# Moving the split weights and the split coefficients to other byte offsets, step by step, in a one-core PEER and mixer kernel

## The chip, the core and the metric

One core of a Trainium2 chip runs the whole kernel as one program. The time is the device time of one execution in microseconds; the kernel before took 1731.04 us, the median of three runs (1727.76, 1731.04, 1736.29).

## The reference, cut to what matters

256 tokens of width 1024 pass through a first block (a mixer, a cross attention, a PEER layer) and a second one (an even mixer, a gated feed-forward, an odd mixer, a second feed-forward). The change lies in the PEER layer. There each token picks, for each of 8 heads, 16 of 128 x 128 experts; an expert is one row of `expert_down` and one of `expert_up`:

```python
u = expert_down[eidx]
a = jax.nn.gelu(jnp.einsum('thkd,td->thk', u, xb), approximate=False)
coef = (g * a.astype(jnp.float32)).astype(xb.dtype)
return jnp.einsum('thk,thkd->td', coef, expert_up[eidx])
```

The kernel computes it densely: for all 16384 experts it takes the product with the token, applies gelu, multiplies with a gate that is zero for the experts not chosen, and multiplies the result with `expert_up`.

## The kernel before, in words

**Three products for one.** Every large product is made in float32r from split operands: a weight piece `raw` (128 partitions x 1024 float32, 4096 bytes in each partition) is loaded by a DMA of SyncE's queue (L418), ScalarE copies it to `hi`, rounded (L430), and VectorE subtracts to get `lo` (L431). The other operand is kept in two halves in the same way. TensorE then makes hi x hi, hi x low half and lo x hi.

**The two expert stages.** In the *down* stage there are 128 steps, one for each first key j. A step (`proj_b`) takes the piece `down[j]` and makes 8 x 3 matmuls (L440, L441, L442): the stationary operand is a 128-column slice of `hi`, `hi`, `lo`; the moving one is the token block `xh`, `xl`, `xh`, 256 columns wide. ScalarE applies gelu (L1207, or L1217 later). In the first part of this stage other work is laid between the steps: first the top-16 search on VectorE, then 64 groups of gate products (L1184 to L1196), which end with 16 small bf16 and fp16 matmuls each (L1192, L1193). In the *output* stage there are again 128 steps (`out_step`, 8 x 3 matmuls at L582, L583, L584): the stationary operand is a slice of `hi`, `hi`, `lo` of `up[j]`; the moving one is the split coefficient of key j, `ch`, `cl`, `ch`, 256 columns each. A coefficient pair (two keys) is made by multiplying gate and gelu (L1244, with gelu values fetched from DRAM, L1243) and splitting (L435, L436) into the tile `u3`.

**Order.** Each engine runs its instructions in a fixed order, and waits on semaphores for the others. A weight tile has three buffers in the expert stages, so a piece is loaded, split and used up to three steps apart.

**Places.** What the change moves is where operands start within a partition. In this text a *place* is the start address in bytes modulo 256. In the kernel before all `raw`, `hi` and `lo` tiles are 4096 bytes long, so that in every buffer of every pool they have one place; in the built program it is 128. The tiles of the moving operands have these places, from the layout of the built program: `xh` and `xl` of the first block and of the down stage 192 and 192; `uh`, `ul` of the pool `xu` (memory projections, PEER queries, even and odd output) 64 and 64, and `u3` 64, so that `ch` and `cl` are at 64 and 64; the token block of the first feed-forward `xh` 64 and `xl` 192, its split activations `uh`, `ul` 64 and 64; the token block of the second feed-forward `xh` 128 and `xl` 0, its `uh`, `ul` 0 and 0. The pools lie one behind the other: `small`, `xu`, a gap of 64 bytes, `w0` (three weight buffers, used in all stages), then `w1` or `w2` (two or three more buffers outside the expert stages), then what a stage needs. A tag's slot has the size of the largest tile with this tag. `skip` puts a small tile in front of a pool and has GpSimd fill it (L399).

Of the kernel before, what the change touches and what calls it, by code (L numbers as in the profile page):

```python
# [11 lines left out]
F32R = mybir.dt.float32r  # L12
# [360 lines left out]
class Builder:  # L373
    def __init__(self, tc, nc, A, out, stages=None):
        self.tc, self.nc, self.A, self.out = tc, nc, A, out
        self.stages = stages
        self.flip = 0
        self.gate = None
        self.free = 100
        self.later = []  # L380
        self.mark = None

    def pool(self, ctx, name, bufs=1, space=None, side=None):
# [13 lines left out]
    def skip(self, pool, nbytes):  # L397
        t = pool.tile([P, nbytes // 4], F32, tag="skip", name="skip", bufs=1)
        self.nc.gpsimd.memset(t, 0.0)  # L399

    def act_set(self, name):
        self.tc.keep_in_program_order(self.nc.scalar.preload_act_table_set(name))
# [7 lines left out]
    def weight(self, ap, width=D, parts=1):  # L410
        nc = self.nc
        i = self.wn % sum(n for _, n in self.wps)
        self.wn += 1
        wp, bufs = self.wps[0] if i < self.wps[0][1] else self.wps[1]
        raw = wp.tile([P, D], F32, tag="raw", name="raw", bufs=bufs)
        cuts = [slice(i * width // parts, (i + 1) * width // parts) for i in range(parts)]
        for c in cuts:
            nc.sync.dma_start(raw[:, c], ap[:, c])  # L418
        hi = wp.tile([P, D], F32R, tag="hi", name="hi", bufs=bufs)
        lo = wp.tile([P, D], F32R, tag="lo", name="lo", bufs=bufs)  # L420
        with ExitStack() as ctx:
            if self.gate:
                self.free -= 1
                if self.free < 0:
                    for ins in self.gate:
                        ctx.enter_context(self.tc.issue_after(ins))
                if self.free < -4:
                    self.gate = None
            for c in cuts:
                nc.scalar.activation(hi[:, c], raw[:, c], AF.Copy)  # L430
                nc.vector.tensor_sub(lo[:, c], raw[:, c], hi[:, c].bitcast(F32))  # L431
        return hi, lo

    def split(self, hi, lo, src):
# [213 lines left out]
    def build(self):  # L648
# [17 lines left out]
        with ExitStack() as ctx:  # L666
# [24 lines left out]
            cw = ExitStack()  # L691
            self.wps = [(base, 3), (self.pool(cw, "w1"), 2)]
            with ExitStack() as c1:
# [32 lines left out]
            with ExitStack() as c2:  # L726
                self.wps = [(base, 3), (self.pool(c2, "w2"), 3)]
                self.op, self.ot = self.xu, "u"
# [352 lines left out]
    def peer(self, xu, base, cw, cx, cq, late, spill, nxt):  # L1081
        nc, A = self.nc, self.A
        mm = nc.tensor.matmul
        with ExitStack() as ctx:
# [119 lines left out]
            while j < P and work:  # L1204
                a = acts_next()
                for i in range(2):
                    self.run(self.proj_b(x, A["down"][j + i], lambda ps: nc.scalar.activation(a[:, i], ps, AF.Gelu),  # L1207
                                         self.tp))
# [5 lines left out]
            for j in range(kept, P):  # L1214
                def ev(ps):
# [3 lines left out]
                    nc.vector.tensor_mul(s, s, a)  # L1219

                self.run(self.proj_b(x, A["down"][j], ev, self.tp))
            cq.close()
# [3 lines left out]
            self.consts(LATE, "c_late")  # L1226
            u1 = self.xu.tile([P, 8, T], F32R, tag="uh", name="u3")
            order = [j for j in range(0, P, 2) if j >= kept] + [j for j in range(GA, P, 2) if j < kept]
# [3 lines left out]
            def step(n):  # L1232
                j = order[n // 2]
                if n % 2 == 0:
# [6 lines left out]
                    if j < kept:  # L1241
                        a = acts_next()
                        nc.sync.dma_start(a.rearrange("p i t -> p (i t)"), store[j // 2])  # L1243
                        nc.vector.tensor_mul(src, src, a)  # L1244
                    i = 4 * (n // 2 % 2)
                    ch, cl = u1[:, i:i + 2], u1[:, i + 2:i + 4]
                    self.split(ch, cl, src)
# [3 lines left out]

            after = Lazy(nxt)
            self.out_proj(step, P, self.h, after, tail=2)
        return after.get()

# [495 lines left out]
```

## Time and profile before

| | before |
|---|---|
| median of three runs | 1731.04 us (1727.76 to 1736.29) |
| profiled execution, its own time | 1739.33 us |
| its span, first to last instruction | 1737.6 us |
| TensorE matmul, busy | 1683.0 us, 97% |
| weight loads, busy | 1602.0 us, 92% |
| VectorE, busy | 1241.1 us, 71% |
| ScalarE, busy | 873.8 us, 50% |
| mean granted TensorE clock | 0.989 |
| down stage (from its first step to the first output step) | 302.40 to 700.74 us |
| output stage (first step to its end) | 700.74 to about 1072 us |

A matmul of 256 columns is listed with about 280 ns, but successive ones start 113 to 119 ns apart, because they overlap. So the busy share says that TensorE always had something in work, and not how fast the stream went. The starts tell that: a step of 24 matmuls lasts from the start of its first one to the start of the next step's first one. Lines are those of the kernel before.

### The profile page before, as it was taken

The numbers are of one execution on the slowest core, as the hardware profiler recorded it, in microseconds if no ns is written. First come the engines' busy times: TensorE is split into PE (matmuls) and PEld (weight loads), VectorE is DVE, ScalarE is ACT, GpSimd is POOL, SyncE is SP. The second block draws the span as 40 slices with busy tenths as digits, with TensorE's granted clock in tenths as the row PEclk, the third lists the DMA queues.
The fourth block names the chain that finished last, engine by engine and source line by source line (L and its number), as shares of the span: only waits on it lengthen the run. The fifth ranks groups of instructions, "written<-read, shape, count | busy, mean of one in ns | idle before, by whom it ended". The sixth has DMA issues, their size and how long they took to land.

```text
span 1737.6 us, 33082 instructions
## 1 busy us (share of the span) xinstructions
PE 1683.0 (97%) x13220; PEld 1602.0 (92%) x13220; DVE 1241.1 (71%) x2309; ACT 873.8 (50%) x1358; POOL 89.1 (5%) x246
## 2 busy tenths in 40 slices
PE   7999999999999999999999999899999999999999
PEld 6879889999999999989999999678999987799998
DVE  6686559998798985678555556686777765677775
ACT  6445345545455554444444446464555454455543
POOL 1011010000000000000000000401100010210000
PEclk9999999999999999999999999999999999999999
DMA  7434454577555655889655556443455544345551
GB/s 263 152 104 147 146 172 131 187 236 260 175 186 199 194 196 188 309 289 299 190 189 186 185 189 210 157 135 110 162 192 186 191 159 155 102 162 190 188 188 62
DMA packets 97516, 318.03 MB, mean 183 GB/s; under 512 B 11841, under 2 KB 13505, under 8 KB 96850
## 3 DMA queue, kind: packets, MB, share of 16 engines
q1 hardware_dynamic: 89154, 301.39, 53.1%
q10 hardware_dynamic: 8208, 14.52, 2.2%
q8 instruction: 104, 1.70, 0.4%
q14 instruction: 50, 0.41, 0.1%
HBM read 299.36 MB, written 16.52 MB: 182 GB/s over the span
## 4 chain that ended last, share of the span: by engine, by line
PE 70%; DVE 7%; DMA 3%; POOL 2%; issue 2%; ACT 1%; SPq 0%; POOLq 0%; DVEq 0%; ACTq 0%
PE tp L440 11%; PE tp L441 11%; PE tp L442 11%; PE acc L582 8%; PE acc L583 8%; PE acc L584 8%; PE acc L440 3%; PE acc L441 3%; DMA u<-store 3%; PE acc L442 3%; DVE lo L431 2%; PE tp L1192 1%; PE tp L1193 1%; DVE ga L1244 1%; DVE w L1345 1%
## 5 line engine op out<-in xcount | busy, mean ns | idle before, releaser
L430 ACT ACTIVATE hi<-raw 128x1024 fp32r<-128x1024 f32 (+1 forms) x533 | 560.2, 1057 | 660.8 <-PE tp L441 246.6
L431 DVE TENSOR_TENSOR lo<-raw,hi 128x1024 fp32r<-128x1024 f32 (+1 forms) x533 | 646.7, 1219 | 309.5 <-ACT hi L430 309.2
L440 PE MATMUL tp<-xh,hi 128*128 128x256 f32 x1680 | 476.7, 284 | 0.6 <-ACT u L1207 0.6
L441 PE MATMUL tp<-xl,hi 128*128 128x256 f32 x1680 | 471.8, 281 | 0.0
L442 PE MATMUL tp<-xh,lo 128*128 128x256 f32 x1680 | 471.1, 280 | 0.6 <-DVE lo L431 0.6
L442 PEld LDWEIGHTS tp<-xh,lo 128*128 128x128 f32 x1680 | 317.1, 189 | 0.8 <-DVE lo L431 0.8
L440 PEld LDWEIGHTS tp<-xh,hi 128*128 128x128 f32 x1680 | 317.0, 189 | 0.8 <-ACT u L1207 0.8
L441 PEld LDWEIGHTS tp<-xl,hi 128*128 128x128 f32 x1680 | 317.2, 189 | 0.0
L583 PE MATMUL acc<-u,hi 128*128 128x256 f32 x1024 | 288.4, 282 | 5.6 <-DVE u L436 5.6
L584 PE MATMUL acc<-u,lo 128*128 128x256 f32 x1024 | 288.2, 281 | 1.4 <-DVE lo L431 1.4
L582 PE MATMUL acc<-u,hi 128*128 128x256 f32 x1024 | 287.9, 281 | 0.0
L583 PEld LDWEIGHTS acc<-u,hi 128*128 128x128 f32 x1024 | 193.0, 188 | 6.4 <-DVE u L436 6.4
L584 PEld LDWEIGHTS acc<-u,lo 128*128 128x128 f32 x1024 | 196.9, 192 | 1.8 <-DVE lo L431 1.8
L582 PEld LDWEIGHTS acc<-u,hi 128*128 128x128 f32 x1024 | 193.0, 189 | 0.0
L440 PE MATMUL acc<-hi,xh 128*128 128x512 f32 (+1 forms) x256 | 103.5, 406 | 1.6 <-ACT y L479 1.6
L441 PE MATMUL acc<-lo,xh 128*128 128x512 f32 (+1 forms) x256 | 101.7, 397 | 0.5 <-DVE lo L431 0.5
L442 PE MATMUL acc<-hi,xl 128*128 128x512 f32 (+1 forms) x256 | 101.1, 395 | 0.0
L582 PE MATMUL acc<-uh,hi 128*128 128x256 f32 x352 | 98.3, 280 | 0.1
L583 PE MATMUL acc<-ul,hi 128*128 128x256 f32 x352 | 98.1, 279 | 0.0
L584 PE MATMUL acc<-uh,lo 128*128 128x256 f32 x352 | 98.1, 279 | 0.0
L457 POOL TENSOR_SCALAR rs_g<-rs_m 128x2 int32<-128x2 int32 (+2 forms) x20 | 10.2, 510 | 1263.8 <-DVE fq L296 810.3
L582 PE MATMUL acc<-oh,hi 128*128 128x256 f32 x256 | 73.1, 285 | 0.0
(436 smaller groups left out, 2801.8 us busy)
## 6 DMA issues: line engine op xcount, KB each, us to landing
raw<-down SPq DMA_DIRECT2D x128, 512.0 KB, 3.7
raw<-up SPq DMA_DIRECT2D x128, 512.0 KB, 4.4
raw<-ffn_up SPq DMA_DIRECT2D x88, 512.0 KB, 3.5
raw<-ffn_down SPq DMA_DIRECT2D x44, 512.0 KB, 3.4
raw<-even_in SPq DMA_DIRECT2D x28, 512.0 KB, 4.4
store<-u ACTq DMA_DIRECT2D x55, 256.0 KB, 3.4
u<-store SPq DMA_DIRECT2D x55, 256.0 KB, 4.7
raw<-odd_in SPq DMA_DIRECT2D x24, 512.0 KB, 3.5
```

Source lines behind the costliest of these rows:

```text
L430: nc.scalar.activation(hi[:, c], raw[:, c], AF.Copy)
L431: nc.vector.tensor_sub(lo[:, c], raw[:, c], hi[:, c].bitcast(F32))
L440: mm(out, lh, rh, start=start, stop=False)
L441: mm(out, lh, rl, start=False, stop=False)
L442: mm(out, ll, rh, start=False, stop=stop)
L582: mm(out, wh[:, cs], oh, start=start and j == 0, stop=False)
L583: mm(out, wh[:, cs], ol, start=False, stop=False)
L584: mm(out, wl[:, cs], oh, start=False, stop=stop and j == 1)
L1192: mm(o, p1[:, b, :, e], hi[:, b, :, e], start=True, stop=False)
L1193: mm(o, p1[:, b, :, e], lo[:, b, :, e], start=False, stop=True)
L1244: nc.vector.tensor_mul(src, src, a)
L1345: nc.vector.match_replace(out=w, in_to_replace=val[:, :8], in_values=s, imm_value=-3e38)
```

## The change

`weight` gives `hi` 64 and `lo` 48 elements more room in pools with three buffers, if `self.lines` is set, and takes its 1024 columns from an offset within that room. In the down stage `line_pair(j)` sets these offsets: that of `hi` goes through eight multiples of 32 bytes, a new one at each step, that of `lo` through seven, a new one every eighth step. In the output stage the offsets are multiples of 64 bytes: `hi` changes every fourth pair of keys, `lo` every sixteenth. `u3` becomes one row of 2144 elements, with `ch` always at one place in either half and `cl` at one of four places, 64 bytes apart, a new one for each pair. `w1` and `w2` get a 64-byte `skip` in front.

From the sizes: a slot of `hi` in `w0` grows from 4096 to 4352 bytes, one of `lo` from 4096 to 4288, the slot of `uh` and `u3` in `xu` from 8192 to 8576.

```diff
+    def skipped(self, ctx, name):
+        pool = self.pool(ctx, name)
+        self.skip(pool, 64)
+        return pool
...
-        hi = wp.tile([P, D], F32R, tag="hi", name="hi", bufs=bufs)
-        lo = wp.tile([P, D], F32R, tag="lo", name="lo", bufs=bufs)
+        if self.lines is None or bufs < 3:
+            hi = wp.tile([P, D], F32R, tag="hi", name="hi", bufs=bufs)
+            lo = wp.tile([P, D], F32R, tag="lo", name="lo", bufs=bufs)
+        else:
+            hi, lo = [wp.tile([P, D + m], F32R, tag=n, name=n, bufs=bufs)[:, o:o + D]
+                      for n, o, m in zip(("hi", "lo"), self.lines, (64, 48))]
...
+    def line_pair(self, j):
+        return tuple(8 * ((v - 4) % 8) for v in (j % 8, (j // 8 % 7 + 4) % 8))
...
-            self.wps = [(base, 3), (self.pool(cw, "w1"), 2)]
+            self.wps = [(base, 3), (self.skipped(cw, "w1"), 2)]
...
-                self.wps = [(base, 3), (self.pool(c2, "w2"), 3)]
+                self.wps = [(base, 3), (self.skipped(c2, "w2"), 3)]
...
                 for i in range(2):
+                    self.lines = self.line_pair(j + i)
                     self.run(self.proj_b(x, A["down"][j + i], lambda ps: nc.scalar.activation(a[:, i], ps, AF.Gelu),
                                          self.tp))
...
+                self.lines = self.line_pair(j)
                 self.run(self.proj_b(x, A["down"][j], ev, self.tp))
...
-            u1 = self.xu.tile([P, 8, T], F32R, tag="uh", name="u3")
+            u1 = self.xu.tile([P, 2144], F32R, tag="uh", name="u3")
...
-                    i = 4 * (n // 2 % 2)
-                    ch, cl = u1[:, i:i + 2], u1[:, i + 2:i + 4]
+                    m = n // 2
+                    self.lines = tuple(16 * ((v - 2) % 4) for v in (m // 4 % 4, m // 16))
+                    wide = u1[:, 1088 * (m % 2):1088 * (m % 2) + 1056 + 32 * (1 - m % 2)]
+                    o = 512 + 16 * ((m - 1) % 4)
+                    ch = wide[:, :512].rearrange("p (i t) -> p i t", i=2)
+                    cl = wide[:, o:o + 512].rearrange("p (i t) -> p i t", i=2)
...
             self.out_proj(step, P, self.h, after, tail=2)
+            self.lines = None
```

## Rows read from the trace of the kernel before

**Rows 1.** The page: busy time, and the chain that ended last.
```profile
PE 1683.0 (97%) x13220; PEld 1602.0 (92%) x13220; DVE 1241.1 (71%) x2309; ACT 873.8 (50%) x1358; POOL 89.1 (5%) x246
...
PE 70%; DVE 7%; DMA 3%; POOL 2%; issue 2%; ACT 1%; SPq 0%; POOLq 0%; DVEq 0%; ACTq 0%
```

**Rows 2.** Busy time by stretch (columns in the heading row), down stage then output stage.
```profile
core 0: us, PE busy (x) PEld busy (x) DVE busy (x) ACT busy (x) POOL busy (x), PEclk, DMA share, GB/s
302.30:401.40 99.10, 97.85 (x827) 97.24 (x826) 92.62 (x350) 49.88 (x73) 0.00 (x0) 1.00 0.68 228
401.40:652.70 251.30, 251.30 (x2368) 248.86 (x2367) 221.32 (x473) 140.14 (x291) 0.00 (x0) 1.00 0.60 195
652.70:700.70 48.00, 48.00 (x410) 48.00 (x409) 27.92 (x36) 23.68 (x36) 0.00 (x0) 1.00 0.59 187
700.70:808.50 107.80, 100.75 (x842) 99.55 (x841) 80.46 (x102) 46.26 (x53) 0.00 (x0) 0.98 0.89 306
808.50:1072.00 263.50, 263.29 (x2235) 262.96 (x2233) 147.06 (x152) 122.79 (x142) 0.00 (x0) 1.00 0.62 198
```

**Rows 3.** Timeline of TensorE: starts of steps far apart, in both expert stages.
```profile
652.69 0.28 PE L440 MATMUL tp<-xh,hi 128*128 128x256 f32 x1
...
697.91 0.28 PE L440 MATMUL tp<-xh,hi 128*128 128x256 f32 x1
...
808.51 0.28 PE L582 MATMUL acc<-u,hi 128*128 128x256 f32 x1
...
1065.73 0.28 PE L582 MATMUL acc<-u,hi 128*128 128x256 f32 x1
```

**Rows 4.** Timeline of TensorE in the output stage, 751 to 811 us: restarts and steps.
```profile
754.21 0.39 PE L583 MATMUL acc<-u,hi 128*128 128x256 f32 x1 [2.31 <-DVE u L436]
...
756.93 0.28 PE L582 MATMUL acc<-u,hi 128*128 128x256 f32 x1
...
759.65 0.28 PE L582 MATMUL acc<-u,hi 128*128 128x256 f32 x1
...
763.28 0.38 PE L584 MATMUL acc<-u,lo 128*128 128x256 f32 x1 [0.52 <-DVE lo L431]
...
765.98 0.28 PE L582 MATMUL acc<-u,hi 128*128 128x256 f32 x1
...
768.80 0.28 PE L582 MATMUL acc<-u,hi 128*128 128x256 f32 x1
```

**Rows 5.** Timeline of TensorE, first feed-forward: output step, then two input steps.
```profile
1244.78 0.28 PE L582 MATMUL acc<-uh,hi 128*128 128x256 f32 x1
...
1247.51 0.28 PE L440 MATMUL tp<-xh,hi 128*128 128x256 f32 x1
...
1250.33 0.28 PE L440 MATMUL tp<-xh,hi 128*128 128x256 f32 x1
...
1253.15 0.28 PE L582 MATMUL acc<-uh,hi 128*128 128x256 f32 x1
```

**Rows 6.** Timeline of TensorE: one output step of the second feed-forward.
```profile
1561.38 0.28 PE L582 MATMUL acc<-uh,hi 128*128 128x256 f32 x1
...
1564.23 0.28 PE L440 MATMUL tp<-xh,hi 128*128 128x256 f32 x1
```

**Rows 7.** Timeline of TensorE: end of the even mixer's output, four steps of matmuls.
```profile
1210.99 0.28 PE L582 MATMUL acc<-oh,hi 128*128 128x256 f32 x1
...
1221.87 0.28 PE L440 MATMUL acc<-xh,hi 128*128 128x256 f32 x1
```

**Rows 8.** Who waited for whom between 401 and 652 us.
```profile
ACT hi L430 <- PE tp L441: 106.7, 73, 2.3
DVE u L1184 <- PE tp L1193: 18.9, 43, 0.8
```

**Rows 9.** GpSimd's fills of skip tiles, by line: count, then min/median/max ns.
```profile
L399 POOL MEMSET skip<- x6: 104/111/118, 0.7 to 1516.7; 128x16 f32 x3, 128x8 f32 x2, 128x24 f32 x1
```

More of the change, by code (lines that the diff above doesn't have):

```diff
@@ L1253, in peer @@
             self.out_proj(step, P, self.h, after, tail=2)
+            self.lines = None
         return after.get()
```

## The prediction

> **What bounds the kernel now.** I read the page first, then busy time by stretch, then the starts of single matmuls. The page puts TensorE at 97% busy and gives it 70% of the chain that ended last; no other engine has over 7% of that chain [rows 1]. By stretch the two expert stages are TensorE's nearly throughout: all 251.30 us of the second part of the down stage, all 48.00 of its end, 263.29 of 263.50 us of the long part of the output stage, at a granted clock of 1.00, the 2.4 GHz level [rows 2]. Busy time can't show whether this stream could go faster, since matmuls overlap. So I count steps of 24 matmuls between two starts. From 652.69 to 697.91 us there are 16 steps, 2.826 us each; from 808.51 to 1065.73 us there are 91, 2.827 us each [rows 3]. That is 117.8 ns a matmul.
>
> This is not the best that the stream does. Between 756.93 and 759.65 us a step of the same stage, same tiles, same places, takes 2.72 us, 113.3 ns a matmul; the one from 765.98 to 768.80 takes 2.82 again [rows 4]. The end of the even mixer's output takes 10.88 us for 96 matmuls, 113.3 ns [rows 7]. So there are two paces, a fast one of 2.720 us and a slow one of 2.827 us a step, 0.107 us apart. What sets them? Two things, by the rows. One is how the stream starts: in the output stage the pace changes only at a wait. It is fast after the restart at 754.21 us and slow after the one at 763.28 [rows 4]; of six restarts there, four were followed by fast steps. The other is place: in the first feed-forward no wait lies between the steps, and yet the output step, whose two moving operands have one place, takes 2.73 us, and the input steps around it, with moving operands at 64 and 192, take 2.82 us, every time [rows 5]. At places 0 and 0 an output step takes 2.85 us [rows 6].
>
> In the expert stages nearly all steps are slow: in the down stage 2 of 128 are fast, in the output stage 12 of 128, all 12 between 751 and 808 us.
>
> **The change part by part.** *Moved operands.* No instruction of TensorE, ScalarE or VectorE in the expert stages is added or removed, none changes its shape, and no DMA changes its size or order. What changes is the place of the weights against the moving operands: `hi` gets a new one at each step of the down stage and every eighth step of the output stage, `cl` one every second step of that stage. The stream's relation, locked for 91 steps now, is then broken again and again. I price a step at one of the two paces, 2.720 or 2.827 us, and ask how many of them will be fast.
>
> Which steps can pay: in the down stage TensorE is busy to the end, and VectorE, with 221.32 of 251.30 us [rows 2], has 30 us in which a faster TensorE isn't held up. It already waits for TensorE's gate products 43 times, 18.9 us [rows 8], so it would start earlier too. From 302 to 401 us VectorE has 92.62 of 99.10 us; 30 steps gain at most 3.2 us there, and 6.5 us are free. So 128 steps of the down stage pay. In the output stage the first 35 steps, 700.70 to 808.50 us, lie in a stretch with a DMA share of 0.89 and 306 GB/s, against 0.62 and 198 after it [rows 2]; TensorE waits there for coefficients whose gelu values come by DMA [rows 4]. What TensorE saves there goes into that wait, and I count it at nothing; were that cover gone it would be up to 23 slow steps x 0.107 = 2.5 us. The other 93 pay. Together 221 steps.
>
> How many turn fast: none can turn below 2.720 us by any row, so the end of the range on one side is 221 x 0.107 = 23.6 us gained; if all went at the worst pace of these rows, 2.85 us [rows 6], 221 x 0.023 = 5 us are lost. For the share I have these: four of six restarts in the output stage; 1 of 64 or so among the restarts after the gate products in the down stage, which are all alike; one of the two places in the first feed-forward; none of those in the second. I take a third, between these ends and nearest to the places without a wait, since a new place without a wait is what the change makes. 221 / 3 = 74 steps, 2 of which are fast already: 72 x 0.107 = 7.7 us gained.
>
> *The rest of the kernel.* The diff moves more than it names. The slot of `uh` in `xu` grows by 384 bytes, so `ul` behind it goes from place 64 to 192, and all of `w0` from 128 to 0; its `lo` buffers then lie 4288 bytes apart and get places 0, 192 and 128. The growth of `w0`, 3 x 256 + 3 x 192 = 1344 bytes, with 384 and the new skip of 64, is 1792, seven times 256, so that everything behind `w1` or `w2` keeps its place. Outside the expert stages three of five or six weight buffers thus have a new place against their moving operands, and the pair in `xu` becomes one of 64 and 192, like the token block of the first feed-forward, which is slow [rows 5]. At stake are some 45 fast steps there (22 output steps of the first feed-forward at 2.73 us, the ends of the even and odd outputs [rows 7], the memory projections and some queries), 45 x 0.107 = 4.8 us if all are lost; and about 200 slow ones, which at the same third would gain 7 us. I take 2 us lost, nearer to the loss, as the pair in `xu` alone carries about 20 of the fast steps (20 x 0.107 = 2.1).
>
> *Added.* Two fills of 64 bytes by GpSimd, 0.11 us each [rows 9]. One stands at the start and one after the output stage, ahead of GpSimd's next work; GpSimd is 5% busy [rows 1]. Nothing; uncovered 0.2 us.
>
> *A rule against the trace.* The rows show two paces, 113.3 and 117.8 ns, at one clock [rows 3, 4]. The Trainium skill (SBUF — State Buffer, Specifications) says that SBUF has 16-byte lines and that an access pays when it crosses to a new one. All places here are multiples of 32 bytes, so by that rule each operand starts on a line as before, and the change gains and loses nothing. Likewise TensorE: Matmul & The Clock Gate (Back-to-back issue gap) gives columns over 2.4 GHz plus 2.5 ns, an estimate of 109 ns for 256 columns at any place, which none of these rows reaches. What would follow from places without effect is the first rival.
>
> **The sum.** 7.7 gained less 2 lost is 5.7 us. Against the profiled execution (1739.33 us, its span 1737.6 with 1.7 around it) that is 1733.6; against the median of the three runs, 1731.04, which lies 8.3 lower, 1725.3. The runs are compared by their medians, so I predict 1725.
>
> **The rivals.** *Place decides nothing, the start of a stream does.* For it: the same places ran at both paces in the output stage [rows 4], and the restarts of the down stage are alike. Against it: the first feed-forward changes pace with place, without a wait [rows 5]. The stages stay slow: 1731, within 3.
>
> *Odd places cost.* Every matmul operand read here in float32r starts at a multiple of 64 bytes now. In the down stage `hi` and `lo` go through multiples of 32, and half of these are odd. If a slice that starts in the middle of 64 bytes takes an access more, and the step falls behind by one more notch of the same 0.107 us, then steps with an odd `hi` or an odd `lo`, 96 of 128, lose 10.3 us, with nothing to cover it, since TensorE is busy throughout [rows 2]. With the 2 us of the other stages, and nothing gained in the even steps, that is 1743. It decides as soon as an odd step loses more than 0.03 us: a third of the output stage's 93 steps and the 32 even ones gains 4.5 us, of which the other stages leave 2.5, and 2.5 over 96 is 0.026. Against it: no row shows such a step, at any pace over 2.85.
>
> *Nearly all turn fast:* each new place shakes the stream out of the slow relation, as four of six restarts did. 200 x 0.107 = 21 less 2: 1712. Against it: the second feed-forward, where two relations alternate and neither is fast [rows 6].
>
> **How the numbers follow.** Forecast 0.48, its own range 1719 to 1734 (a half of the 221 fast with nothing lost elsewhere, a tenth with 4.8 us lost); place without effect 0.27; odd places cost 0.20; nearly all fast 0.05. About 0.5%, 8.7 us, is what a measurement of this kernel can tell from no change: faster means under 1722.4, slower over 1739.7. The forecast gives a little under half of its chance to faster, as its share need be only 0.46 instead of a third for that; with the last rival and a little of the others 0.31. Slower is most of the odd places' 0.20 and a little of the others: 0.20. The rest, 0.49, is within. The range from 1713 to 1745 leaves out about one in six.
>
> **What would show it.** Right: in the output stage after 810 us, steps of 2.72 and 2.83 us in blocks that change with the places, and the same mixed step by step in the down stage; more wait for DMA between 700 and 808 us. Wrong: all steps at 2.83 (first rival); steps over 2.85 us at odd places (second); or fast steps lost outside the expert stages by more than 4.8 us, by the first feed-forward's output steps going to 2.83. A change of instruction order on any engine, or a longer split on ScalarE or VectorE, would upset the argument as a whole.

## The result: 0.6% slower, and two profiles that do not show it

The changed kernel took 1743.97 us (median of 12 runs, 1740.00 to 1750.36), the kernel before 1733.32 us beside it (12 runs, 1726.54 to 1742.28): a ratio of 1.0064, interval 1.0042 to 1.0085, so 10.7 us slower. The prediction was 1725 us, on the other side, with 0.20 on slower. One run of all those named below, of the kernel before beside experiment 12 (1748.14 us), lay in a slower state of the chip and is left out.

The page of the profile after, busy time and the chain that ended last, to be laid beside [rows 1]:

```profile
PE 1687.5 (97%) x13220; PEld 1606.8 (92%) x13220; DVE 1241.9 (71%) x2309; ACT 873.9 (50%) x1358; POOL 89.4 (5%) x248
...
PE 69%; DVE 8%; DMA 3%; POOL 3%; issue 2%; ACT 1%; SPq 0%; POOLq 0%; ACTq 0%; DVEq 0%
```

TensorE has the same 13220 matmuls, and the two added fills of GpSimd are there (246 to 248 instructions). The span is 1738.2 us against 1737.6. These two profiles differ by 0.6 us where the medians differ by 10.7: the profiled execution of the kernel before took 1739.33 us, 6.0 over that kernel's median, and that of the kernel after 1740.00, 4.0 under its own. How far one execution of a kernel lies from another turns out to be half of the story below.

Busy time by stretch (columns as in [rows 2]), the kernel after:

```profile
401.40:652.70 251.30, 251.30 (x2361) 248.75 (x2361) 221.38 (x473) 140.32 (x291) 0.00 (x0) 1.00 0.60 195
652.70:700.70 48.00, 48.00 (x410) 48.00 (x409) 26.85 (x35) 23.69 (x36) 0.00 (x0) 1.00 0.60 186
700.70:808.50 107.80, 103.74 (x867) 102.62 (x866) 82.15 (x104) 46.99 (x54) 0.00 (x0) 1.00 0.90 309
808.50:1072.00 263.50, 262.76 (x2221) 262.39 (x2219) 147.23 (x153) 122.56 (x142) 0.11 (x1) 1.00 0.62 198
```

But for the part with the DMA waits (700.70 to 808.50 us), busy shares, clock, DMA share and rate are nearly those of before. The count of matmuls in a fixed stretch moves: 2361 for 2368, 2221 for 2235 in the part behind the DMA waits, 867 for 842 in the part with them. So the question is again one of starts. Timeline of TensorE, kernel after, output stage (start and length in us, line, operation; each row starts a step of 24 matmuls):

```profile
889.10 0.28 PE L595 MATMUL acc<-u,hi 128*128 128x256 f32 x1
891.98 0.28 PE L595 MATMUL acc<-u,hi 128*128 128x256 f32 x1
...
897.67 0.28 PE L595 MATMUL acc<-u,hi 128*128 128x256 f32 x1
900.41 0.28 PE L595 MATMUL acc<-u,hi 128*128 128x256 f32 x1
...
906.12 0.28 PE L595 MATMUL acc<-u,hi 128*128 128x256 f32 x1
909.04 0.28 PE L595 MATMUL acc<-u,hi 128*128 128x256 f32 x1
```

Without a wait between them, steps take 2.88, 2.74 and 2.92 us. The built program has, with `ch` always at 64, `cl` at 0, 64 and 192 in them, and `hi`, `lo` at 128 and 0 in all three. The down stage of the same kernel:

```profile
447.39 0.28 PE L453 MATMUL tp<-xh,hi 128*128 128x256 f32 x1
450.26 0.28 PE L453 MATMUL tp<-xh,hi 128*128 128x256 f32 x1
453.09 0.28 PE L453 MATMUL tp<-xh,hi 128*128 128x256 f32 x1
455.83 0.28 PE L453 MATMUL tp<-xh,hi 128*128 128x256 f32 x1
```

Here, with the moving operands at 192, `hi` and `lo` at 192 and 192 take 2.87 us, at 224 and 64 2.83, at 0 and 128 2.74. The pace changes with the place, step by step, and the two paces of the prediction are not the only ones: steps go from 2.72 to 2.92 us. Over the stages, in ns from a matmul to the next (starts under 150 ns apart; 24 times this is a step), and the number of steps whose mean lies under or over a bound:

| | down, before | down, after | output, before | output, after |
|---|---|---|---|---|
| mean | 117.75 | 117.96 | 117.34 | 118.23 |
| steps under 115 | 2 | 9 | 13 | 4 |
| steps over 118.5 | 0 | 39 | 1 | 48 |

The output stage is slower by 0.89 ns x 3072 matmuls = 2.7 us of pace, and still 1.7 us shorter in this profile (368.9 against 370.6 us): its gaps of 150 ns and more between two starts come to 5.7 us beyond the pace where they were 10.1. They lie in the part before 808 us; this is the wait behind which the prediction had put the first 35 steps, and it swallows a loss as it would a gain.

Some 1.4 us of that difference is not a wait but TensorE's clock. In the trace of before, the matmuls behind a wait of about 2.3 us at 801.88 start 213 ns apart, 15 of them in a row, and the granted clock of that stretch is far below 1.00 (same columns):

```profile
804.00:808.60 4.60, 4.43 (x24) 4.43 (x25) 4.60 (x7) 1.47 (x3) 0.00 (x0) 0.63 0.93 290
```

So the stretch lies for the most part at the 1.2 GHz level. The trace of after has no such stretch in the two expert stages, and no two starts there are 1.9 us or more apart. It comes back below.

### The profile page after: what moved, and what is told of

Same layout as the page of the kernel before. It is cut to its first block, busy times and chain, and to the rows that moved or that the text cites. A ratio compares the mean times of both kernels' runs of the same rounds, so it can differ in the third digit from the quotient of the medians.

```text
span 1738.2 us, 33083 instructions
## 1 busy us (share of the span) xinstructions
PE 1687.5 (97%) x13220; PEld 1606.8 (92%) x13220; DVE 1241.9 (71%) x2309; ACT 873.9 (50%) x1358; POOL 89.4 (5%) x248
## 4 chain that ended last, share of the span: by engine, by line
PE 69%; DVE 8%; DMA 3%; POOL 3%; issue 2%; ACT 1%; SPq 0%; POOLq 0%; ACTq 0%; DVEq 0%
PE tp L453 11%; PE tp L454 11%; PE tp L455 11%; PE acc L596 8%; PE acc L595 8%; PE acc L597 8%; DMA u<-store 3%; DVE lo L441 3%; PE acc L453 2%; PE acc L454 2%; PE acc L455 2%; PE tp L1205 1%; PE tp L1206 1%; DVE ga L1259 1%; DVE w L1365 1%
## 5 line engine op out<-in xcount | busy, mean ns | idle before, releaser
L597 PEld LDWEIGHTS acc<-u,lo 128*128 128x128 f32 x1024 | 193.0, 188 | 1.3 <-DVE lo L441 1.3
L596 PE MATMUL acc<-ol,hi 128*128 128x256 f32 x256 | 72.4, 283 | 0.0
```

Of the source, the lines that this page charges most:

```text
L596: mm(out, wh[:, cs], ol, start=False, stop=False)
L597: mm(out, wl[:, cs], oh, start=False, stop=stop and j == 1)
```

## The experiments

The kernels below, but for 2, 4 and 11, are the kernel before with this frame, and differ in what `self.lines` holds; the diffs show that, first for the down stage and then for the output stage. The padding of 64 elements on both tiles lengthens `w0` by six times 256 bytes, so with offset 0 every operand of the kernel keeps its place. "Fast" is a step whose mean is under 115 ns.

```diff
+        if self.lines is None or bufs < 3:
             hi = wp.tile([P, D], F32R, tag="hi", name="hi", bufs=bufs)
             lo = wp.tile([P, D], F32R, tag="lo", name="lo", bufs=bufs)
+        else:
+            hi, lo = [wp.tile([P, D + 64], F32R, tag=n, name=n, bufs=bufs)[:, o:o + D]
+                      for n, o in zip(("hi", "lo"), self.lines)]
```

The part on the kernel before says that weights have three buffers in the expert stages. That is not so for the first 54 down steps: they still go round five buffers, three of `w0` and two of `w1`, until the gate products begin (L1170). Offsets act only in pools with three buffers. So in the changed kernel and in every experiment with offsets, 21 of the 128 down steps (two of each five, up to the 54th) keep both weights at 128, and only 107 are moved; in the output stage all 128 are.

**1. The sweep alone.** `hi` and `lo` go through the places of the change; `cl`, the slots and the skips stay as before.

```diff
+                    self.lines = self.line_pair(j + i)
...
+                    self.lines = tuple(16 * ((v - 2) % 4) for v in (m // 4 % 4, m // 16))
```

> Only the offsets of hi and lo in the two expert stages change, by the same rules as in the changed kernel; both get 64 elements of room, so that w0 grows by 1536 bytes, six times 256, and every tile outside these stages, and ch and cl, keep their places. Theory 1 (the sweep itself loses: most places are slow or slower, and a stream that had locked in at the fast pace is broken at the next step): slower than before by most of the 10.6 us, 1740 to 1744, steps between 2.75 and 2.91 us in both stages and hardly any at 2.72. Theory 2 (the loss comes from outside: w0 at place 0 and ul at 192 take the fast steps of the first feed-forward, of the even and of the odd output): within 3 us of before, about 1733, and these steps still at 2.73 us.

Measured: 1740.73 us (1735.88 to 1745.83), ratio 1.0058, interval 1.0039 to 1.0077. The sweep of the weights by itself loses most of what the change loses; 9 down steps and 16 output steps are fast.

**2. The rest alone.** The changed kernel, its slots, skips and padding, with the weights of the expert stages at 128 and `cl` at 64 as before.

```diff
-                      for n, o, m in zip(("hi", "lo"), self.lines, (64, 48))]
+                      for n, o, m in zip(("hi", "lo"), (32, (32, 0, 48)[self.nb % 3]), (64, 48))]
...
-                    o = 512 + 16 * ((m - 1) % 4)
+                    o = 512
```

> All tiles lie as in the changed kernel, but in the expert stages hi and lo are offset so that they start at place 128 in every buffer, and cl stays at place 64: the expert stages as before, the other stages as in the changed kernel. Theory 1 (the sweep loses): within 3 us of before, about 1733. Theory 2 (the other stages lose): 1738 to 1744, with the output steps of the first feed-forward at 2.82 to 2.84 us instead of 2.73. If both shares are real, the sums of the two differences (this one and that of the sweep alone) make the 10.6 us.

Measured: 1732.99 us (1725.16 to 1742.27), ratio 0.9995, interval 0.9971 to 1.002. The trace shows the loss that was foreseen: the 22 output steps of the first feed-forward run at 118.27 ns, none of them fast, where the trace of before has 114.06 ns and 19. Two rows of its timeline, an output step at 1241.68 us, beside the 2.73 us of [rows 5]:

```profile
1241.68 0.28 PE L597 MATMUL acc<-uh,hi 128*128 128x256 f32 x1
...
1244.51 0.28 PE L455 MATMUL tp<-xh,hi 128*128 128x256 f32 x1
```

That is 2.83 us. But over the runs nothing of it can be measured.

**3. Fixed places, 64 bytes to either side.** If the pace belongs to the relation of places, one relation can be held: `hi` 64 bytes above the moving operands, `lo` 64 below, as in the fast steps of the changed kernel. Down: `hi` 0, `lo` 128, moving operands 192. Output: `hi` 128, `lo` 0, moving operands 64.

```diff
+                    self.lines = (32, 0)
...
+                    self.lines = (0, 32)
```

> Fixed places in the expert stages: hi 64 bytes behind the moving operands, lo 64 bytes before them (down stage: x 192, hi 0, lo 128; output stage: ch and cl 64, hi 128, lo 0); all else as before. In the changed kernel the steps with this relation took 2.74 us each of three times in the output stage and 2.74 the one time in the down stage. If the relation of the places sets the pace: 221 steps that pay x 0.087 = 19 us less than before, about 1714, in every execution alike. If the start of a stream sets it: long stretches of one pace, 2.72 or 2.83, as before, and a time within 1726 to 1743.

Measured: 1720.76 us (1715.19 to 1727.27), ratio 0.9937, interval 0.9914 to 0.9961: faster than both kernels. Against the kernel before beside it (1731.99 us) that is 11 us, where 19 were expected. Timeline, starts of steps far apart in both stages:

```profile
643.35 0.28 PE L445 MATMUL tp<-xh,hi 128*128 128x256 f32 x1
...
659.67 0.28 PE L445 MATMUL tp<-xh,hi 128*128 128x256 f32 x1
...
810.51 0.28 PE L587 MATMUL acc<-u,hi 128*128 128x256 f32 x1
...
1041.71 0.28 PE L587 MATMUL acc<-u,hi 128*128 128x256 f32 x1
```

Six down steps take 16.32 us and 85 output steps 231.20, both 2.720 us a step. 115 of 128 down steps and 122 of 128 output steps are fast, also behind the waits before 808 us. Of the others, four down steps stand at 117.5 to 117.7 ns, all of them in the two buffers that are not moved; the rest are broken by a restart or by gate products.

**4 and 11. The kernel before, profiled twice more**, with no edit.

> The kernel before once more, for another profile. If the pace of a stretch is drawn at its start (before's runs spread over 1726.5 to 1742.3, and its profiled execution, at 1739.3, was one of the slow ones), then other stretches of the expert stages are fast this time, and a time near 1730 goes with some 80 to 100 more fast steps. If pace follows from the code alone, the same 14 steps are fast, and time differs for another reason.

> The kernel before, one more look. Theory A (whether a fixed place runs fast is drawn at the start of a stretch): again other steps are fast than in the two looks so far (13 and 19 fast output steps), and the time goes with their count, 0.107 us a step. Theory B (the code decides alone): the same steps as in one of these.

Measured: 1735.99 us and 1728.06 us, one execution each. Both ran 20 down steps in a row fast, 403 to 457 us, which all were slow in the profile that the prediction was made from. Then the second of them, in the output stage, a wait and the steps behind it:

```profile
816.87 0.39 PE L584 MATMUL acc<-u,lo 128*128 128x256 f32 x1 [0.49 <-DVE lo L431]
...
819.49 0.28 PE L582 MATMUL acc<-u,hi 128*128 128x256 f32 x1
...
1050.69 0.28 PE L582 MATMUL acc<-u,hi 128*128 128x256 f32 x1
```

85 steps in 231.20 us, 2.720 each, to the end of the stage. In [rows 3] the same steps of the same program took 2.827. Fast output steps are 13, 19 and 105 in the three profiles, the stage takes 370.6, 368.2 and 359.4 us. So the code alone does not decide; in these output stages a stretch without a wait keeps the pace with which it left its last wait.

The two executions ran on different chips, so the profiles alone don't separate a draw in each execution from a property of the chip. The timed runs speak for a draw. Part of their spread goes with the mean granted clock of the run (in experiments 1, 3, 10 and 12, 0.001 of it with 1.1 to 1.4 us). With that part taken out by a straight line, the runs of the kernel before still scatter by 4.5 to 5.9 us (standard deviation) on each of four chips, those of experiment 2, which has its places, by 5.4; those of experiments 1, 3, 5, 6, 10 and 12, whose output stage sweeps, holds another relation or is started fast, by 1.3 to 2.3. (Experiments 7, 8 and 9 below: 7.7, 3.2 and 2.6.) That the scatter is one of paces stays unshown: timed runs show no stages.

**5. The same place for all.** As 3, with `hi` and `lo` at the place of the moving operands.

```diff
+                    self.lines = (16, 16)
...
+                    self.lines = (48, 48)
```

> Fixed places as in e3_fixed_apart, but hi and lo both at the place of the moving operands (192 in the down stage, 64 in the output stage). Theory A (the distance between the place of the weights and that of the moving operands sets the pace, and equal places are the bad end of it): the output steps run near the 119.8 and 120.1 ns per matmul that the changed kernel showed for them, the down steps on the base pool near 119; (107 x 24 x 1.5 ns) + (128 x 24 x 2.6 ns) = 12 us above the kernel before, ratio about 1.007, no fast steps. Theory B (a place only decides whether fast stretches can begin, none is slower than 117.8): at most the few fast stretches of before are lost, ratio 1.000 to 1.002.

Measured: 1748.13 us (1745.23 to 1749.79), ratio 1.0079, interval 1.0048 to 1.0111. Timeline, both stages:

```profile
661.20 0.28 PE L445 MATMUL tp<-xh,hi 128*128 128x256 f32 x1
...
678.48 0.28 PE L445 MATMUL tp<-xh,hi 128*128 128x256 f32 x1
...
826.74 0.28 PE L587 MATMUL acc<-u,hi 128*128 128x256 f32 x1
...
1071.54 0.28 PE L587 MATMUL acc<-u,hi 128*128 128x256 f32 x1
```

6 down steps in 17.28 us and 85 output steps in 244.80, both 2.880 us a step, 120.0 ns, a pace that no row of the kernel before has. No output step is fast. Theory A holds for the steps that were moved. But 19 down steps are fast, all among the 21 in buffers that were not moved, with both weights 64 below the moving operands. Timeline, a moved step, two unmoved ones and the start of the next:

```profile
309.03 0.28 PE L445 MATMUL tp<-xh,hi 128*128 128x256 f32 x1
...
311.91 0.28 PE L445 MATMUL tp<-xh,hi 128*128 128x256 f32 x1
...
314.63 0.28 PE L445 MATMUL tp<-xh,hi 128*128 128x256 f32 x1
...
317.35 0.28 PE L445 MATMUL tp<-xh,hi 128*128 128x256 f32 x1
```

2.88, 2.72 and 2.72 us, with no wait between them, and so again in nearly every round of five. In the trace of before all 21 of these steps, at the same places, took the slow pace. So a change of place without a wait can also set the pace of the next place, and a slow stretch ahead does not always hand on a slow one.

**6. The good relation, 32 bytes further.**

```diff
+                    self.lines = (40, 8)
...
+                    self.lines = (8, 40)
```

> The places of e3_fixed_apart with 32 bytes added to both (down: hi 32, lo 160; output: hi 160, lo 32; moving operands as before at 192 and 64). Theory A (32 bytes take a step off the fast pace: in the changed kernel odd places had 118.3 to 118.6 ns and hardly a fast step): no fast steps, 235 steps x 24 x 0.8 ns = 4.5 us above before, ratio 1.001 to 1.004. Theory B (only that hi and lo lie about 128 bytes apart, on the two sides of the moving operands): as e3_fixed_apart, ratio 0.994, more than 200 fast steps.

Measured: 1739.04 us (1735.80 to 1740.54), ratio 1.0032, interval 1.0008 to 1.0056. Output steps of its timeline, nine of them:

```profile
821.92 0.28 PE L587 MATMUL acc<-u,hi 128*128 128x256 f32 x1
...
847.36 0.28 PE L587 MATMUL acc<-u,hi 128*128 128x256 f32 x1
```

25.44 us, 2.827 each: the slow pace of before, and not one output step is fast. No moved step of either stage is fast, as theory A has it. So this odd relation costs the fast pace and, in the output stage, adds nothing to the slow one. In the down stage the mean is 117.73 ns, with 60 steps over 118.5: those between gate products run at 118.9, which is 0.027 us a step over the slow pace. The 17 fast down steps are all in the buffers that were not moved.

**7. `hi` and `lo` exchanged.**

```diff
+                    self.lines = (0, 32)
...
+                    self.lines = (32, 0)
```

> e3_fixed_apart with the places of hi and lo exchanged (down: hi 128, lo 0; output: hi 0, lo 128). Theory A (hi and lo 128 bytes apart is what counts, whichever is which): ratio 0.994, nearly all steps at 113.3 to 114 ns. Theory B (hi has to lie 64 bytes above the moving operands and lo 64 below; the changed kernel showed 118.9, 113.3 and 118.8 ns for the exchanged pair in the output stage): most steps at 117.8 or above, ratio 1.000 to 1.003.

Measured: 1733.42 us (1721.71 to 1745.46), ratio 0.9998, interval 0.9965 to 1.0031. In its trace:

```profile
822.40 0.28 PE L587 MATMUL acc<-u,hi 128*128 128x256 f32 x1
...
848.08 0.28 PE L587 MATMUL acc<-u,hi 128*128 128x256 f32 x1
```

Nine output steps take 25.68 us, 2.853 each; yet 66 down steps and 14 output steps are fast. Which of `hi` and `lo` lies above matters, as theory B has it, though this relation too has more than one pace, and the runs spread over 24 us.

**8 and 9. The sweep in one stage each**, the first line in 8 and the second in 9; the other stage has (0, 0), its places of before.

```diff
+                    self.lines = self.line_pair(j + i)
...
+                    self.lines = tuple(16 * ((v - 2) % 4) for v in (m // 4 % 4, m // 16))
```

> The sweep of hi and lo in the down stage alone, everything else at the places of before. The sweep in both stages alone cost a ratio of 1.0058. If the loss is shared by the steps as their mean pace in the changed kernel has it (down +0.21 ns, output +0.89 ns per matmul): 1.001 to 1.002 here, the rest in the output stage. If the odd places, which only the down stage visits, carry the loss: 1.004 to 1.006.

> The sweep of hi and lo in the output stage alone, in steps of 64 bytes, everything else at the places of before. Theory A (at a fixed place the output stage is in some executions fast for a long stretch, 360 us against 371 for the stage, and the sweep takes these away; the sweep in the down stage cost nothing): the whole loss of the changed kernel is here, ratio 1.004 to 1.008, and the runs lie closer together than those of before (1723 to 1743), about 1735 to 1746. Theory B (the loss of the sweep needs both stages): ratio under 1.003.

Measured: the down sweep 1732.13 us (1727.90 to 1748.06), ratio 0.9999, interval 0.9972 to 1.0025; the output sweep 1737.54 us (1731.79 to 1747.78), ratio 1.0051, interval 1.0027 to 1.0076. The loss that the runs show lies in the output stage, where no odd place occurs; the 1.004 to 1.006 that odd places were to cost lies outside the interval of the down sweep. In the down stage the trace has a small one: the 76 moved steps with an odd place run at 118.3 ns and none is fast, the 31 moved steps with even places at 117.3 with 5 fast; experiment 1 and the changed kernel have the same within 0.3 ns. The down sweep's own output stage, at the places of before, shows what is at stake there:

```profile
824.72 0.28 PE L590 MATMUL acc<-u,hi 128*128 128x256 f32 x1
...
1055.92 0.28 PE L590 MATMUL acc<-u,hi 128*128 128x256 f32 x1
```

85 steps, 2.720 us each, fast to the end (114 of 128; the first 14 are slow). And the output sweep, where places change every eighth step:

```profile
822.01 0.28 PE L587 MATMUL acc<-u,hi 128*128 128x256 f32 x1
...
842.17 0.28 PE L587 MATMUL acc<-u,hi 128*128 128x256 f32 x1
...
890.39 0.28 PE L587 MATMUL acc<-u,hi 128*128 128x256 f32 x1
...
909.43 0.28 PE L587 MATMUL acc<-u,hi 128*128 128x256 f32 x1
...
914.98 0.28 PE L587 MATMUL acc<-u,hi 128*128 128x256 f32 x1
```

Seven steps in 20.16 us (2.88 each), seven in 19.04 (2.72), then two in 5.55, the second of which is 2.827. The pace turns with the first matmuls of a new place. From the starts, the median ns a matmul in each block, moving operands at 64:

| | `lo` 0 | `lo` 64 | `lo` 128 | `lo` 192 |
|---|---|---|---|---|
| `hi` 0 | 117.8 | 117.8 | 113.3 | 115.5 |
| `hi` 64 | 117.8 | 120.0 | 117.8 | 119.2 |
| `hi` 128 | 113.4 | 117.8 | 117.8 | 118.2 |
| `hi` 192 | 116.7 | 118.3 | 117.8 | 118.7 |

The mean of these 16 is 117.4. Experiment 1 passed the same blocks with the same medians within 0.1 ns.

**10. The good relation in the later stages too.** As 3, with `hi` at 128 and `lo` at 0 behind the output stage and all moving operands there at 64.

```diff
+                self.lines = (0, 32)
...
-            return lambda: Norm(self, self.h, i, self.xq, off=16 if i == 8 else 0)
+            return lambda: Norm(self, self.h, i, self.xq, off=0)
...
-            self.skip(mp, 32 if l else 96)
+            self.skip(mp, 96)
```

> e3_fixed_apart, and in the stages behind the output stage too the moving operands at 64, hi at 128 and lo at 0. Theory A (the relation of places sets the pace in every stage): the steps of the two feed-forward layers, the even and the odd stage go from about 117.8 to 113.5 ns; some (984 + 1012 + 526) x 4.2 ns = 10.6 us and a little below e3_fixed_apart, about 1709, ratio 0.986 to 0.989. Theory B (what decides lies in the expert stages' own stream, long runs with no other work between): as e3_fixed_apart, 0.993 to 0.995.

Measured: 1707.21 us (1702.23 to 1715.82), ratio 0.9874, interval 0.9837 to 0.9911. An output step and an input step of the second feed-forward, beside the 2.85 us of [rows 6]:

```profile
1533.28 0.28 PE L587 MATMUL acc<-uh,hi 128*128 128x256 f32 x1
1536.00 0.28 PE L445 MATMUL tp<-xh,hi 128*128 128x256 f32 x1
1538.72 0.28 PE L445 MATMUL tp<-xh,hi 128*128 128x256 f32 x1
```

2.72 us each. The input steps of both feed-forwards go from 117.7 and 117.8 ns to 113.4, the output steps of the second from 118.37 to 113.49. The relation acts in the later stages too; the stages ahead of the PEER layer were not tried.

**12. Does a stretch keep its pace?** The places of before, but `lo` at 0 in the first 48 output steps; the down stage has (0, 0).

```diff
+                    self.lines = (0, 32 if m < 24 else 0)
```

> The places of before everywhere, but for the first 48 of the 128 output steps lo lies at 0 instead of 128, which makes them fast wherever the trace has shown that pair (hi 128, lo 0, moving operands at 64). The last 80 steps lie behind the last wait of the stage and have the places of before. Theory A (a stretch without a wait keeps the pace that it came with, fast or slow, at the places of before): these 80 run at 113.3 ns in the profile, the output stage takes about 360 us, and the runs have lost the slow half of those of before: ratio 0.994 to 0.998, about 1722 to 1730. Theory B (the pace at a place does not depend on what ran ahead of it): the 80 steps run at 117.8 ns from the first one on, only the 48 gain, at most 48 x 0.107 = 5 us, most of it in waits; ratio 0.998 to 1.001.

Measured: 1731.34 us (1726.52 to 1735.40), ratio 0.9982, interval 0.9951 to 1.0012. Timeline; `lo` changes place at 844.63 us:

```profile
839.19 0.28 PE L587 MATMUL acc<-u,hi 128*128 128x256 f32 x1
...
844.63 0.28 PE L587 MATMUL acc<-u,hi 128*128 128x256 f32 x1
847.35 0.28 PE L587 MATMUL acc<-u,hi 128*128 128x256 f32 x1
...
1054.07 0.28 PE L587 MATMUL acc<-u,hi 128*128 128x256 f32 x1
```

The first step at the places of before takes 2.72 us, and the 76 behind it 206.72, 2.720 each, where [rows 3] has 2.827. In experiment 9 the same places, entered from a slow block, ran at 117.8 ns for all eight steps. So theory A holds for the pace: in the output stage, with both weights at 128, the stream stays as it came. (In the unmoved down steps of experiment 5 both weights lie 64 below the moving operands, and there it did not.) In time the gain is not distinguishable from none: the stage took 364.3 us, not 360, as its waits over 0.3 us sum to 13.5 us (8.8 in profile 11), and behind the longest of them the clock fell (columns: TensorE busy, granted clock, DMA share, GB/s):

```profile
803.68 0.58 PE L588 MATMUL acc<-u,hi 128*128 128x256 f32 x1 [2.79 <-DVE u L441]
...
803.68:809.81 6.13, 6.13 (x29) 0.51 0.88 265
```

In it 26 matmuls start 213 ns apart instead of 113, 2.6 us lost; profile 11 has no such stretch. The runs lie within 9 us of each other, those of before beside them within 22 (1720.27 to 1742.31).

## Why the prediction was wrong

**The step that failed** is "How many turn fast ... I take a third". Of the 256 expert steps of the changed kernel 13 were fast, not 74, and 87 ran at over 118.5 ns. Five of the 13 are down steps whose weights were not moved at all. (The kernel before had 15: two down steps and 13 output steps, of which the prediction counted 12.) The share was taken from places that happened to be in the kernel before; a sweep visits all of them, and their mean is 117.4 ns with `cl` held (experiment 9) and 118.23 with `cl` swept too, which is the slow pace and no gain. (In the changed kernel `lo` also has another place in each buffer.) The good relations are 2 of 16; equal places, at 120.0, undo one of them. The count of steps that could pay was off too: the 128 down steps include the 21 that stay in place, so it was 107 + 93 = 200, not 221; a third of that would still have been a forecast of a gain.

**The bound on the slow side** was too small for the same reason. I took 2.85 us as the worst, since no row had more; a step at equal places takes 2.88 (experiment 5), the worst seen 2.92. A bound from the rows of one layout does not bound another layout.

**"The stream's relation, locked for 91 steps now, is then broken"** was read as a gain. The lock is real, but it holds either pace, and executions differ in which; the scatter of the runs fits a draw in each. Five profiled executions had the output stage at the places of before (the kernel before three times, experiments 2 and 8): 370.6, 368.2, 359.4, 369.3 and 360.4 us, mean 365.6. Three had it swept (the changed kernel, experiments 1 and 9): 368.9, 371.1 and 368.9, mean 369.6. I argued from the slowest of the five. The sweep gives up the fast stretches and gets the mean of the places, 4.0 us more. The down stage took 396.9 us on average at the places of before (six executions, 396.2 to 398.3, with experiments 9 and 12 and without 8) and 399.4 swept (399.2 to 399.5), 2.5 us more. By stage lengths that is 6.5 us of the 10.7, whose interval is 7.3 to 14.7. By pace alone it is more, since the waits take no part: the five output stages had a mean of 115.93 ns, the changed kernel's 118.23, and 2.30 x 3072 = 7.1 us; the down stages 117.07 and 117.92, 2.6 us; together 9.7. Which of the two the runs follow was not settled: profiles are few, stage lengths hold waits and stretches at the 1.2 GHz level that come and go, and runs that were only timed show no stages. So that the sweep loses is shown (experiments 1 and 9), while the size of the loss rests on five profiles against three.

**The rest of the kernel**, 2 us lost: the fast steps went where I said (experiment 2), the price by the runs is 0.9 us gained, with an interval from 5.0 gained to 3.5 lost, so its sign can't be told. **The added fills** cost nothing that shows. **What can pay** held for the output stage: with nearly all its steps fast it is 10.3 us shorter than in the first profile (360.3 us, experiment 3), against 93 x 0.107 = 10.0. The down stage gains 8.2 us (390.1), less than 128 x 0.107 = 13.7: four steps stayed slow and nine more held a restart or gate products, and its gaps of 150 ns and more went from 65 with 7.0 us beyond the pace to 86 with 10.1. All the new ones lie before 401 us, where I had called 6.5 us of VectorE's free: a faster stream is held up there. One wait of TensorE in experiment 3 between 300 and 700 us (who waits for whom, total us, times, longest):

```profile
PE tp L445 <- ACT u L1213: 2.0, 1, 2.0
```

By the profile it waits for ScalarE's gelu, which reads the accumulator that TensorE writes next; the longest such wait in the trace of before is 0.6 us. Behind it the clock falls here too, and 15 matmuls start 213 ns apart, so that a wait of 2.0 us costs 1.5 us more (columns as in experiment 12):

```profile
336.57:339.93 3.36, 3.36 (x18) 0.51 0.32 122
```

This term is not in the prediction: a faster stream meets longer waits, and what it gained can go into the clock behind them. It is not certain to. In the expert stages of all traces 13 times two starts lie 2.1 us or more apart (up to 3.3); eight of these were followed by such a stretch, and those of 2.43, 2.59, 2.77, 2.84 and 2.88 us were not.

**The rivals.** *Place decides nothing* falls with experiments 3, 5 and 10. *Odd places cost* came nearest in time, 1743, and by luck: the stage with the odd places lost nothing measurable when swept alone (0.9999, 0.9972 to 1.0025), the one without them lost 1.0051. Its notch of 0.107 us a step did not come: a whole output stage at one odd relation runs at 117.8 ns (experiment 6), and the 76 moved down steps with an odd place (not 96) lie 0.02 us over the even ones. An odd place costs the chance of the fast pace, and held throughout that is measurable (1.0032, 1.0008 to 1.0056). *Nearly all turn fast* describes experiment 3, which gets it by holding one relation instead of changing it.

**The rule weighed.** The Trainium skill (SBUF — State Buffer, Specifications) makes an access pay when it crosses to a new 16-byte line. Experiments 3 and 5 both start all operands on multiples of 64 bytes and run at 113.3 and 120.0 ns; the measurement decides, and that rule does not reach this effect. The estimate of 109 ns from the Trainium skill (TensorE: Matmul & The Clock Gate, Back-to-back issue gap), which the page gives for single matmuls and not for a stream with weight loads, was reached by no stretch of 24 such matmuls in any run; the best is 113.3.

**What stays open** is the mechanism: no run shows what it is in the reads of weights and moving operands that takes longer. The runs show only that the distances of the places go with the pace, that one relation was fast wherever it was held (`hi` 64 above, `lo` 64 below: experiments 3, 10, 12), one was slow in every moved step (all equal, experiment 5), and at least three have two paces: both weights 64 above; both 64 below (113.3 and 117.8 ns, the down stage of before); and `hi` 64 below with `lo` 64 above (113.3 ns in experiment 9; 113.3 and 118.9 in 7). What picks one of the two is not known: a wait, a few steps at another relation, and an unmoved step in between each did it in some trace.

## What to carry to other kernels

When TensorE is busy throughout, take the starts of matmuls in long stretches and compare them with the best stretch of the same shape; a gap of 4% with no wait in it can be one of operand addresses, and here it was got by finding one good relation and holding it, not by varying it. Before reading anything into one profile, see where its own time lies among the runs, and profile the same kernel a second time: a pace that differs between profiles does not follow from the code alone. Check which buffers a change of layout really reaches. And a mean over all variants of a thing is no better than its average member, so a sweep pays only where the present choice is below that.

## What the runs showed of the hardware

- A float32r product of three matmuls with 256 columns each, back to back at a granted clock of 1.00 (the 2.4 GHz level), ran at 113.3 to 120.0 ns a matmul in steady stretches, depending on where weights and moving operands start (given here modulo 256 bytes); that is 6% between the same instructions on the same data sizes (experiments 3 and 5).
- A stretch without a wait can hold one of two paces at the same places, for 85 steps and more; it changed behind a wait of 0.49 us in profile 11, and 48 steps at a good relation ahead of it set it in experiment 12.
- Moving the good relation by 32 bytes takes the fast pace away: 0 of 128 output steps fast (experiment 6) against 122 (experiment 3).
- Behind waits of TensorE of 2.0 us (experiment 3) and 2.79 us (experiment 12) the granted clock was 0.51, the 1.2 GHz level, for 3.4 and 6.1 us, and matmuls started 213 ns apart; other waits of that length had no such stretch behind them.
- Where the pace is fixed, a lower mean granted clock of a run goes with a longer time: 1702.23 us at 0.994 and 1715.82 at 0.982 in experiment 10.
